# Readout of the second tile with values stationary, parts dealt evenly, and moved exponentials in a two-layer decoder trunk

## The chip, the cores and the metric

The kernel runs on one core of a Trainium2 chip. The metric is the device time of one execution in microseconds (us). TensorE (PE) multiplies matrices and turns tiles over (transposes), and loads each stationary operand with a weight load (PEld); VectorE (DVE), ScalarE (ACT) and GpSimd (POOL) work elementwise; SyncE (SP) issues the DMAs. Each engine takes its instructions in the order in which they are written and waits at an instruction until its semaphores are set. SBUF holds the tiles, PSUM has eight banks of 128 x 512 words into which PE writes.

## The reference, cut to what matters

```python
x <- LayerNorm(alpha * x + gated_deltanet(x))       # layer 1
shared keys and values of three branches from x      # compressed, selected, window
# layer 2, per head h of 16 and token t of 256 (heads in groups of 4 share keys and values):
q = rope(x @ wq); z = x @ wz (3 x 1024); gates = sigmoid(x @ wg)
o_b = softmax(q k_b^T, masked) v_b                   # b = compressed, selected, window
o = sum_b gates_b * o_b * silu(z_b)
x <- LayerNorm(alpha * x + o @ w_out)
```

With 256 tokens the selected and the window branch read the same 256 positions with different masks.

## The kernel before, in words

All products run in about 32 bits on PE: a projection is three products (high by high, high by low, low by high part), so a weight block is cast to its high part on ACT (`hi_*`, L181) and its low part is made on POOL (`lo_*`, L185).

The change lies in the second layer, from about 221 us of the span to its end. There the 256 tokens are two tiles of 128. The attention is cut into 24 units: a unit of tile 0 is a pair of heads (keys 0 to 127 only), a unit of tile 1 is one head (all 256 keys). The string `UNITS` gives their order, "0" for tile 0, "1" for tile 1. One unit is this chain: scores `s` (PE) into one of two score banks; `maxima` with the mask (DVE); `exps` (ACT) into `pt`; `transposes` of `pt` into the bank `ptp` (PE); copy to `PT` (ACT, `probs`); `readout` into the bank `op` (PE), where `PT` is stationary and the values with a column of ones (65 columns, `vtok`) stream, and a small product with `vbd` reads the compressed branch; five DVE instructions, here called the gated sums (L1418 to L1422), which divide by the sum in the ones column, multiply by gate and `zz`, and add the branches. `zz` is silu of z, made by `bz_done`: `th` on ACT, then `zz` on DVE.

Between scores and transposes of a unit, and between transposes of one and scores of the next, PE gets other work, so that the chain has time: `fill(n)` emits n parts of the projections (a part of `bz` or `bo` for tile 0 is six products of 512 columns, for the last sums of tile 1 twelve of 256). `FA` says how many parts stand ahead of a unit's exponentials, `FB` how many behind its readout and ahead of its transposes. The order on every engine is the order in which the program emits, `defer(n, f)` emits f at the n-th `step` after it, and each `fill` steps once for a part.

Two banks are shared with one buffer each: tag "t" (`tbank`: `ptp`, `qtp`, `tp_b`) and tag "o" (`obank`: `op`). Who asks for the bank waits until the last reader of its former content is done. The two score banks (`sbank`) also serve `gp` and `gq`, the gates' products.

The last steps: `merge` turns the summed heads over (`tp_b`) and splits them (`x1h`, `x1l`), then the parts of `bo` run, and the layer norm (`ln_part`, `ln_affine`) ends the kernel.

Of the kernel before, what the change touches and what calls it, by code (L numbers as in the profile page):

```python
# [9 lines left out]
F32 = mybir.dt.float32  # L10
# [24 lines left out]

FIRST = (1, 2)

UNITS = "001010101101101101111111"
FA = "3113111011210212044211123"
FB = "0211121311122110212111000"  # L40

PRE, TAIL = 4, 2
NEG = -1e30
# [50 lines left out]
def trunk(ctx: ExitStack, tc: tile.TileContext, I: dict, out: bass.AP):  # L94
# [9 lines left out]
    def defer(n, f):  # L104
        late.append([n, f])
# [802 lines left out]
    def ln_part(t, w, lo, ps, xin, dst):  # L908

        if lo == 0:  # L910
            stt[w, t] = [sm.tile([P, 4, 6], F32, tag="st", name=f"st_{w}{t}"), 0]
        st, n = stt[w, t]
        cc = slice(lo, lo + ps.shape[-1])
        V.scalar_tensor_tensor(dst[:, cc], xin[:, cc], SQRT2, ps, op0=ALU.mult, op1=ALU.add)
        V.bn_stats(st[:, n, :], dst[:, cc])
        stt[w, t][1] += 1

    def ln_mean(t, w):
# [6 lines left out]

    def ln_affine(t, w, b, dst, store=None, src=None):
        mv = ln_mean(t, w)
        if src:

            for c in range(2):  # L930
                V.scalar_tensor_tensor(src[c], src[c], mv[:, 0:1], lnp[w][:, c * 512:c * 512 + 512],
                                       op0=ALU.subtract, op1=ALU.mult)
            for c in range(2):
                cc = slice(c * 512, (c + 1) * 512)
                V.scalar_tensor_tensor(dst[:, cc], src[c], mv[:, 1:2], lnp[b][:, cc], op0=ALU.mult, op1=ALU.add)
            return
        for c in range(2):
            cc = slice(c * 512, (c + 1) * 512)
            V.scalar_tensor_tensor(dst[:, cc], dst[:, cc], mv[:, 0:1], lnp[w][:, cc], op0=ALU.subtract, op1=ALU.mult)
        for c in range(2):  # L940
            cc = slice(c * 512, (c + 1) * 512)
            V.scalar_tensor_tensor(dst[:, cc], dst[:, cc], mv[:, 1:2], lnp[b][:, cc], op0=ALU.mult, op1=ALU.add)
            if store:
                store(cc)
# [83 lines left out]
    def obank(name):  # L1028
        return pt_.tile([P, 512], F32, tag="o", name=name)
# [209 lines left out]
    def zview(t, c0, n):  # L1239
        i, o = c0 // 1536, c0 % 1536  # L1240
        return zz[2 * t + i][:, o:o + n]

    def need_z(t, cols):
        while not all((c, t) in zdone for c in range(-(-cols // 512))):
            fill(1)
# [12 lines left out]
    add_pairs(48)  # L1258
    S.copy(wgs[:, :, 0:48], wg)
    G.tensor_tensor(wgs[:, :, 48:96], wg, wgs[:, :, 0:48].bitcast(F32), op=ALU.subtract)  # L1260
    fill(1)
    r = q_split()
    fill(1)
    compressed_v()
    for i in range(4):
        if i:
# [54 lines left out]
    order0 = [(0, h) for h in range(0, 16, 2)]  # L1321
    order1 = [(1, h) for h in range(16)]
    units = [order0.pop(0) if k == "0" else order1.pop(0) for k in UNITS]
    S_, PT_, PTT, PC, PCT, MX, TP = {}, {}, {}, {}, {}, {}, {}
    cnt = {"n": 0}

    def scores(u):
# [26 lines left out]
    def exps(u):  # L1354
        t, h = u
        sp, mx = S_[u], MX[u]
        s4 = sp[:, :, 0:256].rearrange("p j (b k) -> p j b k", b=2)
        pt = PT_[u] = wk.tile([P, 2, 2, P], F32, tag="hl", name=f"pt{t}{h}", bufs=3)
        if t == 0 or h % 2 == 0:
            PC[t, h] = wk.tile([P, 2, 16], F32, tag="Pc", name=f"Pc{t}{h}", bufs=4)  # L1360
        Pc = PC[t, h - h % 2]
        if t == 0:
            for j in range(2):
                for b in range(2):
                    S.activation(pt[:, j, b, :], s4[:, j, b, :], AF.Exp, bias=mx[:, 2 * j + b:2 * j + b + 1])
                S.activation(Pc[:, j, :], sp[:, j, 256:272], AF.Exp, bias=mx[:, 4 + j:5 + j])
        else:
            for b in range(2):
                S.activation(pt[:, :, b, :], s4[:, :, b, :], AF.Exp, bias=mx[:, b:b + 1])  # L1369
            S.activation(Pc[:, h % 2, :], sp[:, 0, 256:272], AF.Exp, bias=mx[:, 4:5])  # L1370

    def transposes(u):
        t, h = u
# [16 lines left out]

    OP, summed = {}, set()

    def readout(t, h, half=None):

        g_ = h // 4
        if half != 1:
            need_z(t, (h + 2) * 192)
            OP[t] = obank(f"op{t}{h}")
        o3 = OP[t][:, 0:390].rearrange("p (r b d) -> p r b d", r=2, b=3)
        for r in range(2) if half is None else (half,):  # L1400
            PT = PTT[0, h] if t == 0 else PTT[1, h + r]
            for b in range(2):
                if t == 0:
                    PE.matmul(o3[:, r, 1 + b, :], PT[:, r, b, :], vt_[:, b, 0, g_, :], start=True, stop=True)
                else:
                    for j in range(2):
                        PE.matmul(o3[:, r, 1 + b, :], PT[:, j, b, :], vt_[:, b, j, g_, :], start=j == 0, stop=j == 1)  # L1407
        if half == 0:
            return
        PE.matmul(o3[:, :, 0, :], PCT[t, h], vbd[:, g_, :, :], start=True, stop=True)  # L1410
        rc = sm.tile([P, 2, 3], F32, tag="rc", name=f"rc{t}{h}")
        o4 = o3[:, :, :, 0:64]

        o_ = zview(t, h * 192, 128).rearrange("p (r d) -> p r d", r=2)

        def total():

            V.reciprocal(o3[:, :, :, 64], o3[:, :, :, 64])  # L1418
            V.tensor_tensor(rc, o3[:, :, :, 64], gt[:, t, h * 3:h * 3 + 6].rearrange("p (r b) -> p r b", b=3), op=ALU.mult)
            V.tensor_tensor(o4, o4, zview(t, h * 192, 384).rearrange("p (r b d) -> p r b d", r=2, b=3), op=ALU.mult)  # L1420
            V.tensor_tensor(o4, o4, rc[:, :, :, None].to_broadcast([P, 2, 3, 64]), op=ALU.mult)
            V.tensor_reduce(o_, o4.rearrange("p r b d -> p r d b"), axis=AX.X, op=ALU.add)  # L1422
            summed.add((t, h))

        defer(1, total)
# [17 lines left out]
    def bo_unit(t, c, part):  # L1443
        if part == 0:
            pb_[t, c] = [(sbank(f"pbl{c}{f}")[:, 0] if c else pjb(f"pbl{c}{f}")) for f in range(2)] if t else pjb(f"pbo{c}{t}")
        if t == 0 and c == 1 and part == 1:
            for nm in ("blw", "blb"):
                load_ln(nm, ring.tile([P, D], F32, tag="raw", name=nm, bufs=NRAW))
        x = x1[:, t, :]

        def store(cc):
            nc.sync.dma_start(out[t * P:(t + 1) * P, cc], x[:, cc])

        def done(lo, ps):
            ln_part(t, "blw", lo, ps, x, x)
            if lo + ps.shape[-1] == D:
                (ln_affine if t else ln_affine_aside)(t, "blw", "blb", x, store)

        if t == 1:

            for f in range(2):
                ps = pb_[t, c][f][:, 0:256]
                tm_part(ps, ("bo", 4 * c + part), part, t, *bT, cols=slice(256 * f, 256 * f + 256))
                if part == 3:
                    done(512 * c + 256 * f, ps)
            return
# [28 lines left out]
    for i in range(n + 1):  # L1495
        if i < n:
            scores(units[i])
        first = i < n and units[i][0] == 0 and not merges
        if first:

            maxima(units[i])
        if i:
            probs(units[i - 1])
        step()
        if i < n and not first:
            maxima(units[i])
        fill(int(FA[i]))
        advance()
        presplit()
        if i < n:  # L1510
            exps(units[i])
        if i:
            t, h = units[i - 1]
            if t == 0:
                readout(t, h)
                if h == 14:
                    cnt["t0"] = 1
                    merges += [lambda: merge0(0), lambda: merge0(1)] + ready
            else:

                if (units[i - 2] if h % 2 else units[i]) == (1, h ^ 1):
                    readout(t, h - h % 2, h % 2)
                elif h % 2:
                    readout(t, h - 1)
                if h % 4 == 3:
                    (merges if cnt["t0"] else ready).append(lambda g_=h // 4: merge1(g_))
        fill(int(FB[i]))
        if i < n:
            transposes(units[i])
    while len(merges) > 1:  # L1530
# [78 lines left out]
```

## Time and profile before

| | us |
|---|---|
| median of 3 runs | 386.9 (386.45 to 387.45) |
| profiled execution | 388.53 |
| its span, first to last instruction | 386.8 |
| PE busy | 374.7 (97%) |
| DVE, ACT, POOL busy | 223.6, 220.4, 247.1 |
| mean granted TensorE clock | 0.993 of full speed |

The profiled execution is 1.7 us longer than its span and 1.6 us longer than the median; busy shares are means over the whole span. Matmuls overlap in the records, so that the time that one adds to PE's row is read from start to start. In rows of the timeline, instructions of one kind that follow one another are one row with their count.

### The profile page before, as it was taken

What the parts mean: (1) busy time and instruction counts of PE and PEld (TensorE: products, weight loads), DVE (VectorE), ACT (ScalarE), POOL (GpSimd) and SP (SyncE); (2) the same over time, 40 slices, a digit from 0 to 9 for tenths busy, and PEclk for the clock granted to TensorE, in tenths of its full rate; (3) what the DMA queues carried; (4) which work ended last, traced back from release to release, by engine and by line L of the source; (5) the groups of instructions that cost most, each with busy time, mean ns of one, the idle gap of its engine ahead of it and who ended that gap; (6) DMA issues with size and microseconds to landing.
All of it is one profiled execution on the core that took longest, in us unless ns stands there. A gap on an engine that the chain in (4) does not pass through costs nothing.

```text
span 386.8 us, 7558 instructions
## 1 busy us (share of the span) xinstructions
PE 374.7 (97%) x2870; PEld 332.9 (86%) x2870; DVE 223.6 (58%) x591; ACT 220.4 (57%) x433; POOL 247.1 (64%) x157
## 2 busy tenths in 40 slices
PE   8899999999999999999999999999999999999991
PEld 6899999999888987888897878888888888878991
DVE  2777876588642543656542545754557456677726
ACT  4687785546854543535563567675664757456410
POOL 5499999837456747895854997474736547209051
PEclk9999999999999999999999999999999999999997
DMA  6776749845433316384545854433516143301011
GB/s 223 292 218 208 268 158 297 228 167 143 148 109 112 110 54 200 128 287 147 169 158 166 297 195 159 164 111 109 173 45 218 55 153 113 117 3 54 3 54 54
DMA packets 23476, 58.68 MB, mean 152 GB/s; under 512 B 6672, under 2 KB 9232, under 8 KB 23312
## 3 DMA queue, kind: packets, MB, share of 16 engines
q1 hardware_dynamic: 23232, 58.13, 45.1%
q8 instruction: 22, 0.36, 0.4%
q14 instruction: 14, 0.11, 0.1%
q10 hardware_dynamic: 144, 0.07, 0.1%
q0 software_dynamic: 64, 0.01, 0.0%
HBM read 55.96 MB, written 2.23 MB: 150 GB/s over the span
## 4 chain that ended last, share of the span: by engine, by line
PE 90%; DMA 3%; DVE 2%; POOL 1%; ACT 1%; issue 1%; POOLq 0%; SPq 0%; DVEq 0%
PE pbz L235 6%; PE pbz L233 6%; PE pbz L234 6%; PE op L1407 4%; PE s L1336 3%; PE ptp L1378 3%; PE pwz L233 2%; PE pk L217 2%; PE pwo L235 2%; PE pq L216 2%; PE pq L215 2%; PE pq L217 2%; PE pk L215 2%; PE pk L216 2%; PE pwo L234 2%; PE pwo L233 2%
## 5 line engine op out<-in xcount | busy, mean ns | idle before, releaser
L185 POOL TENSOR_TENSOR lo_bz<-raw_bz,hi_bz 128x1024 fp32r<-128x1024 f32 x24 | 56.8, 2392 | 36.2 <-ACT hi_bz L181 19.6
L185 POOL TENSOR_TENSOR lo_wqkv<-raw_wqkv,hi_wqkv 128x1024 fp32r<-128x1024 f32 x22 | 52.5, 2406 | 7.9 <-ACT hi_wqkv L181 6.1
L233 PE MATMUL pbz<-hi_bz,x1h 128*128 128x512 f32 x96 | 38.7, 403 | 0.0
L235 PE MATMUL pbz<-lo_bz,x1h 128*128 128x512 f32 x96 | 37.8, 394 | 0.0
L234 PE MATMUL pbz<-hi_bz,x1l 128*128 128x512 f32 x96 | 37.6, 392 | 0.0
L185 POOL TENSOR_TENSOR lo_bo<-raw_bo,hi_bo 128x1024 fp32r<-128x1024 f32 x8 | 18.9, 2387 | 21.7 <-ACT hi_bo L181 16.9
L185 POOL TENSOR_TENSOR lo_skv<-raw_skv,hi_skv 128x1024 fp32r<-128x1024 f32 x12 | 28.4, 2397 | 4.2 <-PE pskv L235 4.2
L185 POOL TENSOR_TENSOR lo_wz<-raw_wz,hi_wz 128x1024 fp32r<-128x1024 f32 x8 | 19.4, 2438 | 16.0 <-ACT hi_wz L181 10.6
L181 ACT CAST hi_bz<-raw_bz 128x1024 fp32r<-128x1024 f32 x24 | 25.3, 1052 | 2.5 <-POOL wgs L1260 1.6
L185 POOL TENSOR_TENSOR lo_bq<-raw_bq,hi_bq 128x1024 fp32r<-128x1024 f32 x8 | 19.1, 2393 | 11.6 <-ACT hi_bq L181 7.2
L185 POOL TENSOR_TENSOR lo_wo<-raw_wo,hi_wo 128x1024 fp32r<-128x1024 f32 x8 | 18.9, 2385 | 11.9 <-ACT hi_wo L181 11.9
L1385 ACT COPY PT<-ptp 128x512 f32<-128x512 f32 x24 | 14.1, 588 | 21.2 <-PE ptp L1378 21.2
L181 ACT CAST hi_wqkv<-raw_wqkv 128x1024 fp32r<-128x1024 f32 x22 | 22.8, 1043 | 2.4 <-DMA raw_wqkv<-in_wqkv 2.4
L235 PEld LDWEIGHTS pbz<-lo_bz,x1h 128*128 128x128 f32 x96 | 18.0, 188 | 4.3 <-POOL lo_bz L185 0.2
L234 PEld LDWEIGHTS pbz<-hi_bz,x1l 128*128 128x128 f32 x96 | 18.1, 188 | 2.8
L233 PEld LDWEIGHTS pbz<-hi_bz,x1h 128*128 128x128 f32 x96 | 18.1, 188 | 2.8
L1369 ACT ACTIVATE pt<-s,mx 128x256 f32<-128x256 f32 x32 | 13.4, 471 | 10.9 <-DVE mx L1352 8.7
L217 PE MATMUL pk<-xh,lo_wqkv 128*128 128x256 f32 x64 | 18.2, 285 | 0.9 <-POOL lo_wqkv L185 0.9
L215 PE MATMUL pk<-xh,hi_wqkv 128*128 128x256 f32 x64 | 18.6, 290 | 0.0
L215 PE MATMUL pq<-xh,hi_wqkv 128*128 128x256 f32 x64 | 18.5, 289 | 0.0
L216 PE MATMUL pk<-xl,hi_wqkv 128*128 128x256 f32 x64 | 18.1, 283 | 0.0
L217 PE MATMUL pq<-xh,lo_wqkv 128*128 128x256 f32 x64 | 18.1, 283 | 0.0
(362 smaller groups left out, 1257.9 us busy)
## 6 DMA issues: line engine op xcount, KB each, us to landing
raw_bz<-in_bz SPq DMA_DIRECT2D x24, 512.0 KB, 3.3
raw_wqkv<-in_wqkv SPq DMA_DIRECT2D x23, 512.0 KB, 4.4
raw_skv<-in_skv SPq DMA_DIRECT2D x12, 512.0 KB, 3.3
raw_wz<-in_wz SPq DMA_DIRECT2D x8, 512.0 KB, 3.9
raw_wo<-in_wo SPq DMA_DIRECT2D x8, 512.0 KB, 3.6
raw_bq<-in_bq SPq DMA_DIRECT2D x8, 512.0 KB, 3.6
raw_bo<-in_bo SPq DMA_DIRECT2D x8, 512.0 KB, 3.3
raw_w<-in_w SPq DMA_DIRECT2D x4, 512.0 KB, 3.3
```

The costliest lines, as they stand in the source:

```text
L181: S.copy(h, r)
L185: e.tensor_tensor(l, r, h.bitcast(F32), op=ALU.subtract)
L215: PE.matmul(ps[:, 0:T], wh[:, kt, :], ah[:, kt, :], start=kt == 0, stop=False)
L216: PE.matmul(ps[:, 0:T], wh[:, kt, :], al_[:, kt, :], start=False, stop=False)
L217: PE.matmul(ps[:, 0:T], wl[:, kt, :], ah[:, kt, :], start=False, stop=kt == 7)
L233: PE.matmul(ps, ah[:, kt, tt], wh[:, k4, cols], start=kt == 0, stop=False)
L234: PE.matmul(ps, al_[:, kt, tt], wh[:, k4, cols], start=False, stop=False)
L235: PE.matmul(ps, ah[:, kt, tt], wl[:, k4, cols], start=False, stop=kt == 7)
L1336: PE.matmul(sp[:, j, 0:n], lq, kk[:, hh // 4, c0:c0 + n], start=i == 0, stop=i == 1)
L1369: S.activation(pt[:, :, b, :], s4[:, :, b, :], AF.Exp, bias=mx[:, b:b + 1])
L1385: S.copy(PT.rearrange("p a b c -> p (a b c)"), TP[u])
L1407: PE.matmul(o3[:, r, 1 + b, :], PT[:, j, b, :], vt_[:, b, j, g_, :], start=j == 0, stop=j == 1)
```

## The change

It does six things.

1. `UNITS`, `FA` and `FB` are new tables: nearly every unit has one or two parts ahead of its readout and one behind.
2. The readout of tile 1 (`readout_rows`) has the values stationary (64 columns) and `PT` streaming (128 columns): eight products for a pair of heads, which fill the lower and upper half of the partitions of a "t" bank by turns. DVE copies the result to `oS`. In the next unit, behind its first part, `turn_back` turns `oS` over with two transposes into the "o" bank and adds the product with `vbd`.
3. The sums of the softmax of tile 1 come from the exponentials (`accum_out`, 48 instructions) in place of the ones column.
4. `exps` stands ahead of the weights' cast (`presplit`), and for units of tile 0 up to the merges right behind `maxima`, ahead of what `step` emits.
5. The first `q_split` stands ahead of two parts instead of between them.
6. For tile 1, the first 512 columns of the last sums stay in their two banks until the last layer norm has read them.

```diff
-UNITS = "001010101101101101111111"
-FA = "3113111011210212044211123"
-FB = "0211121311122110212111000"
+UNITS = "001101100111011100111111"
+FA = "3112121111111111111222213"
+FB = "0111111111111111101010100"
...
-        V.scalar_tensor_tensor(dst[:, cc], xin[:, cc], SQRT2, ps, op0=ALU.mult, op1=ALU.add)
-        V.bn_stats(st[:, n, :], dst[:, cc])
+        y = ps if dst is None else dst[:, cc]
+        V.scalar_tensor_tensor(y, xin[:, cc], SQRT2, ps, op0=ALU.mult, op1=ALU.add)
+        V.bn_stats(st[:, n, :], y)
...
-        for c in range(2):
-            cc = slice(c * 512, (c + 1) * 512)
-            V.scalar_tensor_tensor(dst[:, cc], dst[:, cc], mv[:, 0:1], lnp[w][:, cc], op0=ALU.subtract, op1=ALU.mult)
+        for c, y in enumerate(src):
+            cc = slice(c * 256, (c + 1) * 256)
+            V.scalar_tensor_tensor(dst[:, cc], y, mv[:, 0:1], lnp[w][:, cc], op0=ALU.subtract, op1=ALU.mult)
+        cc = slice(512, 1024)
+        V.scalar_tensor_tensor(dst[:, cc], dst[:, cc], mv[:, 0:1], lnp[w][:, cc], op0=ALU.subtract, op1=ALU.mult)
...
-    fill(1)
     r = q_split()
-    fill(1)
+    fill(2)
...
+            den = DEN[h - h % 2]
             for b in range(2):
-                S.activation(pt[:, :, b, :], s4[:, :, b, :], AF.Exp, bias=mx[:, b:b + 1])
-            S.activation(Pc[:, h % 2, :], sp[:, 0, 256:272], AF.Exp, bias=mx[:, 4:5])
+                S.activation(pt[:, :, b, :], s4[:, :, b, :], AF.Exp, bias=mx[:, b:b + 1],
+                             accum_out=den[:, h % 2, 1 + b:2 + b])
+            S.activation(Pc[:, h % 2, :], sp[:, 0, 256:272], AF.Exp, bias=mx[:, 4:5], accum_out=den[:, h % 2, 0:1])
...
+    def readout_rows(h):
+
+
+        g_ = h // 4
+        tb = tbank(f"ot{h}")
+        for r in range(2):
+            for j in range(2):
+                for b in range(2):
+                    PE.matmul(tb[64 * b:64 * b + 64, r * P:(r + 1) * P], vt_[:, b, j, g_, 0:64], PTT[1, h + r][:, j, b, :],
+                              start=j == 0, stop=j == 1)
+        oS = wk.tile([P, 2, P], F32, tag="oS", name=f"oS{h}", bufs=1)
+        V.tensor_copy(oS.rearrange("p a b -> p (a b)"), tb[:, 0:2 * P])
+        backs.append(lambda: turn_back(h, oS))
+
+    def turn_back(h, oS):
+        need_z(1, (h + 2) * 192)
+        op = OP[1] = obank(f"op1{h}")
+        o3 = op[:, 0:384].rearrange("p (r b d) -> p r b d", r=2, b=3)
+        for r in range(2):
+            PE.transpose(op[:, r * 192 + 64:r * 192 + 192], oS[:, r, :], ident)
+        PE.matmul(o3[:, :, 0, :], PCT[1, h], vbd[:, h // 4, :, 0:64], start=True, stop=True)
+        defer(1, lambda: gated(1, h, o3, DEN[h]))
...
+        if first:
+            exps(units[i])
         step()
         if i < n and not first:
             maxima(units[i])
-        fill(int(FA[i]))
+
+        k = 1 if merges else 0
+        if backs:
+            fill(1)
+            turn()
+            fill(int(FA[i]) - 1 - k)
+        else:
+            fill(int(FA[i]) - k)
         advance()
+        fill(k)
+        if i < n and not first:
+            exps(units[i])
         presplit()
-        if i < n:
-            exps(units[i])
         if i:
             t, h = units[i - 1]
             if t == 0:
-                readout(t, h)
+                readout(h)
...
-                if (units[i - 2] if h % 2 else units[i]) == (1, h ^ 1):
-                    readout(t, h - h % 2, h % 2)
-                elif h % 2:
-                    readout(t, h - 1)
+                if h % 2:
+                    readout_rows(h - 1)
```

In the changed kernel the gated sums are L1407 to L1411, the readout of tile 0 is L1422 and L1423, that of tile 1 L1436, the copy to `oS` L1439, the turning back L1447 and L1448, and the exponentials of tile 0 are L1369 and L1370.

The order on ACT at the start of the weave, before: the last two casts of queries, the table of the exponential with the gates' exponential, a weight block's cast, `th` of the first part, then the first unit's exponentials.

```order
L1224 CAST qT_2696<-qtp_3059 128x4x128
L1224 CAST qT_2696<-qtp_3064 128x4x128
L1310 ACT_TABLE_LOAD
L1310 ACTIVATE gq<-gq 128x96
L181 CAST hi_bz_3090<-raw_bz_2935 128x1024
L1236 ACTIVATE th_3101<-pbz_3004 128x512
L1365 ACTIVATE pt_3117<-s_3072,mx_3077 128x128 x2
L1366 ACTIVATE Pc_3118<-s_3072,mx_3077 128x16
L1365 ACTIVATE pt_3117<-s_3072,mx_3077 128x128 x2
L1366 ACTIVATE Pc_3118<-s_3072,mx_3077 128x16
```

And with the change:

```order
L1369 ACT_TABLE_LOAD
L1369 ACTIVATE pt_3081<-s_3072,mx_3077 128x128 x2
L1370 ACTIVATE Pc_3082<-s_3072,mx_3077 128x16
L1369 ACTIVATE pt_3081<-s_3072,mx_3077 128x128 x2
L1370 ACTIVATE Pc_3082<-s_3072,mx_3077 128x16
L1227 CAST qT_2696<-qtp_3059 128x4x128
L1227 CAST qT_2696<-qtp_3064 128x4x128
L1312 ACTIVATE gq<-gq 128x96
L181 CAST hi_bz_3098<-raw_bz_2935 128x1024
L1239 ACTIVATE th_3109<-pbz_3004 128x512
```

The table and the first unit's exponentials have moved ahead of the casts of the queries, the gates' exponential and `th`.

The order on PE around the scores of the last pair of tile 0 (`s_4030` before, `s_4019` after), before: the readout of a tile-1 pair (`op_4014`), the transposes of the unit ahead, then the scores; two parts and the transposes follow (rows 1715 to 1727, not shown).

```order
L1407 MATMUL op_4014<-vtok,PT_3871 128x65 x4
L1407 MATMUL op_4014<-vtok,PT_3973 128x65 x4
L1410 MATMUL op_4014<-vbd,PcT_2388 128x2x65
L1378 MATMUL ptp_4025<-ident,pt_4009 128x128 x4
L1336 MATMUL s_4030<-kh,qT_2696 128x272
L1336 MATMUL s_4030<-kl,qT_2696 128x272
```

With the change, from the last half of the part behind the scores:

```order
L233 MATMUL pbz_4042<-hi_bz_3622,x1h 128x512
L234 MATMUL pbz_4042<-hi_bz_3622,x1l 128x512
L235 MATMUL pbz_4042<-lo_bz_3623,x1h 128x512
L1447 MATMUL op_4049<-ident,oS_4005 128x128 x2
L1448 MATMUL op_4049<-vbd,PcT_2388 128x2x64
L1422 MATMUL op_4059<-vtok,PT_4028 128x65 x4
L1423 MATMUL op_4059<-vbd,PcT_2389 128x2x65
L1384 MATMUL ptp_4065<-ident,pt_4031 128x128 x4
L1386 MATMUL s_4019<-ident,Pc_4032 32x128
```

The turning back of a tile-1 pair (`op_4049`) and the readout of a tile-0 pair (`op_4059`) now stand side by side, and both ask for the one "o" bank.

The order on DVE at the same place, before: maxima of that unit, the gated sums of `op_4014`, maxima of the next unit.

```order
L1345 TENSOR_TENSOR s_4030<-s_4030,cb 128x2x272
L1346 TENSOR_REDUCE mx_4035<-s_4030 128x4
L1347 TENSOR_REDUCE mx_4035<-s_4030 128x2
L1418 RECIPROCAL op_4014<-op_4014 128x6
L1419 TENSOR_TENSOR rc_4024<-op_4014,gt 128x6
L1420 TENSOR_TENSOR op_4014<-op_4014,zz_3273 128x6x64
L1421 TENSOR_TENSOR op_4014<-op_4014,rc_4024 128x6x64
L1422 TENSOR_REDUCE zz_3273<-op_4014 128x128
L1349 TENSOR_TENSOR s_4072<-s_4072,cb 128x256
```

With the change, from the last of the maxima on:

```order
L1240 SCALAR_TENSOR_TENSOR zz_3598<-th_4039,pbz_3931 128x512
L1407 RECIPROCAL op_4049<-den_3883 128x6
L1408 TENSOR_TENSOR rc_4079<-op_4049,gt 128x6
L1409 TENSOR_TENSOR op_4049<-op_4049,zz_3922 128x384
L1410 TENSOR_TENSOR op_4049<-op_4049,rc_4079 128x384
L1411 TENSOR_REDUCE zz_3922<-op_4049 128x128
L1407 RECIPROCAL op_4059<-op_4059 128x6
L1408 TENSOR_TENSOR rc_4085<-op_4059,gt 128x6
L1409 TENSOR_TENSOR op_4059<-op_4059,zz_3598 128x6x64
L1410 TENSOR_TENSOR op_4059<-op_4059,rc_4085 128x6x64
L1411 TENSOR_REDUCE zz_3598<-op_4059 128x128
L1351 TENSOR_TENSOR s_4071<-s_4071,cb 128x256
```

DVE now has `zz` and then two runs of gated sums one behind the other, and the second run reads the bank that PE writes only when the first is done.

## Rows read from the trace of the kernel before

**Rows 1.** The page, part 4: shares of the chain that ended last, by engine.
```profile
PE 90%; DMA 3%; DVE 2%; POOL 1%; ACT 1%; issue 1%; POOLq 0%; SPq 0%; DVEq 0%
```

**Rows 2.** Windows: length; busy us of PE, PEld, DVE, ACT, POOL; granted clock; DMA.
```profile
232.00:332.00 100.00, 100.00 (x599) 87.21 (x598) 57.24 (x134) 63.85 (x142) 58.11 (x25) 1.00 0.40 132
332.00:346.00 14.00, 13.08 (x87) 10.83 (x86) 12.05 (x32) 7.19 (x21) 0.00 (x0) 1.00 0.10 39
```

**Rows 3.** Timeline, first units with a readout: start us, us, engine, line, operation, [idle before].
```profile
246.03 0.40 PE L233 MATMUL pbz<-hi_bz,x1h 128*128 128x512 f32 x1
...
247.41 1.00 PE L1404 MATMUL op<-vtok,PT 128*128 128x65 f32 x8
247.60 0.18 DVE L1347 TENSOR_REDUCE mx<-s 128x2 f32<-128x32 f32 x1
247.90 0.62 ACT L1365 ACTIVATE pt<-s,mx 128x128 f32<-128x128 f32 x2 [1.55 <-DVE mx L1347]
...
248.73 0.20 DVE L1418 RECIPROCAL op<-op 128x6 f32<-128x6 f32 x1 [0.94 <-PE op L1410]
...
249.07 0.30 ACT L1366 ACTIVATE Pc<-s,mx 128x16 f32<-128x16 f32 x1
...
250.12 0.60 ACT L1236 ACTIVATE th<-pbz 128x512 f32<-128x512 f32 x1 [0.75 <-PE pbz L235]
...
250.37 0.56 DVE L1422 TENSOR_REDUCE zz<-op 128x128 f32<-128x384 f32 x1
...
250.84 0.68 DVE L1237 SCALAR_TENSOR_TENSOR zz<-th,pbz 128x512 f32<-128x512 f32 x1
```

**Rows 4.** Timeline of PE, one readout of a pair of tile 1.
```profile
271.36 1.89 PE L1407 MATMUL op<-vtok,PT 128*128 128x65 f32 x16
273.09 0.44 PE L1410 MATMUL op<-vbd,PcT 128*128 128x130 f32 x2
...
273.60 0.40 PE L234 MATMUL pbz<-hi_bz,x1l 128*128 128x512 f32 x1
```

**Rows 5.** Timeline, a column-tiled block (L1150, the keys' and values' compression).
```profile
207.17 0.39 PE L235 MATMUL pbq<-lo_bq,x1h 128*128 128x512 f32 x1
...
207.48 1.72 PEld L1150 LDWEIGHTS hpT<-raw_w,C 128*61 128x61 f32 x32 [0.35 <-issue]
...
209.38 0.50 PE L233 MATMUL pbq<-hi_bq,x1h 128*128 128x512 f32 x1
...
209.72 0.39 PE L234 MATMUL pbq<-hi_bq,x1l 128*128 128x512 f32 x1
```

**Rows 6.** Timeline, the first unit of the weave: ACT and DVE.
```profile
239.68 1.07 ACT L1224 CAST qT<-qtp 128x512 fp32r<-128x512 f32 x2 [0.20 <-PE qtp L1223]
...
240.78 1.28 ACT L1310 ACT_TABLE_LOAD   x1
...
242.07 0.23 ACT L1310 ACTIVATE gq<-gq 128x96 f32<-128x96 f32 x1
...
243.93 0.24 DVE L1315 TENSOR_SCALAR gt<-gq,cb 128x16 f32<-128x16 f32 x1
```

**Rows 7.** Timeline, the first turning of queries (L1223).
```profile
223.38 0.66 PE L1223 MATMUL qtp<-ident,hlq 128*128 128x128 f32 x4 [0.54 <-DVE hlq L1048]
```

**Rows 8.** Timeline, small POOL operations in two layer norms, layer 1's and the last.
```profile
155.73 0.23 POOL L922 TENSOR_SCALAR mv_alw<-mv_alw 128x1 f32<-128x1 f32 x1 [3.05 <-DVE mv_alw L921]
...
156.04 0.57 POOL L923 TENSOR_TENSOR mv_alw<-mv_alw,mhalf 128x1 f32<-128x1 f32 x1
...
380.44 0.78 POOL L922 TENSOR_SCALAR mv_blw<-mv_blw 128x1 f32<-128x1 f32 x1 [6.70 <-DVE mv_blw L921]
381.30 0.93 POOL L923 TENSOR_TENSOR mv_blw<-mv_blw,mhalf 128x1 f32<-128x1 f32 x1
```

**Rows 9.** Busy time behind PE's last matmul, as in rows 2.
```profile
380.00:381.00 1.00, 0.00 (x0) 0.00 (x0) 0.93 (x3) 0.00 (x0) 0.56 (x1) 1.00 0.00 0
381.00:382.00 1.00, 0.00 (x0) 0.00 (x0) 0.80 (x2) 0.00 (x0) 0.92 (x2) 0.82 0.00 0
```

More of the change, by code (lines that the diff above doesn't have):

```diff
@@ L927, in ln_affine @@
         mv = ln_mean(t, w)
-        if src:
+        if src and not store:
             for c in range(2):
@@ L1323, in trunk @@
     units = [order0.pop(0) if k == "0" else order1.pop(0) for k in UNITS]
-    S_, PT_, PTT, PC, PCT, MX, TP = {}, {}, {}, {}, {}, {}, {}
+    S_, PT_, PTT, PC, PCT, MX, TP, DEN = {}, {}, {}, {}, {}, {}, {}, {}
     cnt = {"n": 0}
@@ L1360, in exps @@
             PC[t, h] = wk.tile([P, 2, 16], F32, tag="Pc", name=f"Pc{t}{h}", bufs=4)
+            if t:
+                DEN[h] = sm.tile([P, 2, 3], F32, tag="den", name=f"den{h}", bufs=3)
         Pc = PC[t, h - h % 2]
@@ L1391, in trunk @@
     OP, summed = {}, set()
-    def readout(t, h, half=None):
-        g_ = h // 4
[L1396 to L1401, printed above, removed]
-            for b in range(2):
[L1403 to L1425, printed above, removed]
@@ new lines, in gated @@
+    def gated(t, h, o4, den):
+        rc = sm.tile([P, 2, 3], F32, tag="rc", name=f"rc{t}{h}")
+        o_ = zview(t, h * 192, 128).rearrange("p (r d) -> p r d", r=2)
+        rd = OP[t][:, 0:390].rearrange("p (r b d) -> p r b d", r=2, b=3)[:, :, :, 64] if t == 0 else \
+            OP[t][:, 384:390].rearrange("p (r b) -> p r b", r=2)
+        V.reciprocal(rd, den)
+        V.tensor_tensor(rc, rd, gt[:, t, h * 3:h * 3 + 6].rearrange("p (r b) -> p r b", b=3), op=ALU.mult)
+        V.tensor_tensor(o4, o4, zview(t, h * 192, 384).rearrange("p (r b d) -> p r b d", r=2, b=3), op=ALU.mult)
+        V.tensor_tensor(o4, o4, rc[:, :, :, None].to_broadcast([P, 2, 3, 64]), op=ALU.mult)
+        V.tensor_reduce(o_, o4.rearrange("p r b d -> p r d b"), axis=AX.X, op=ALU.add)
+        summed.add((t, h))
@@ new lines, in readout @@
+    def readout(h):
+        g_ = h // 4
+        need_z(0, (h + 2) * 192)
+        OP[0] = obank(f"op0{h}")
+        o3 = OP[0][:, 0:390].rearrange("p (r b d) -> p r b d", r=2, b=3)
+        for r in range(2):
+            for b in range(2):
+                PE.matmul(o3[:, r, 1 + b, :], PTT[0, h][:, r, b, :], vt_[:, b, 0, g_, :], start=True, stop=True)
+        PE.matmul(o3[:, :, 0, :], PCT[0, h], vbd[:, g_, :, :], start=True, stop=True)
+        defer(1, lambda: gated(0, h, o3[:, :, :, 0:64], o3[:, :, :, 64]))
@@ new lines, in trunk @@
+    backs = []
+    def readout_rows(h):
[9 more added lines that the diff above has]
+        backs.append(lambda: turn_back(h, oS))
@@ L1428, in trunk, with turn @@
+    def turn_back(h, oS):
+        need_z(1, (h + 2) * 192)
+        op = OP[1] = obank(f"op1{h}")
+        o3 = op[:, 0:384].rearrange("p (r b d) -> p r b d", r=2, b=3)
+        for r in range(2):
+            PE.transpose(op[:, r * 192 + 64:r * 192 + 192], oS[:, r, :], ident)
+        PE.matmul(o3[:, :, 0, :], PCT[1, h], vbd[:, h // 4, :, 0:64], start=True, stop=True)
+        defer(1, lambda: gated(1, h, o3, DEN[h]))
+    def turn():
+        while backs:
+            backs.pop(0)()
     bT = x1h, x1l
@@ L1454, in done @@
         def done(lo, ps):
-            ln_part(t, "blw", lo, ps, x, x)
+            inb = t == 1 and lo < 512
+            ln_part(t, "blw", lo, ps, x, None if inb else x)
             if lo + ps.shape[-1] == D:
-                (ln_affine if t else ln_affine_aside)(t, "blw", "blb", x, store)
+                if t:
+                    ln_affine(t, "blw", "blb", x, store, [p[:, 0:256] for p in pb_[1, 0]])
+                else:
+                    ln_affine_aside(t, "blw", "blb", x, store)
         if t == 1:
@@ L1506, in trunk @@
             maxima(units[i])
-        fill(int(FA[i]))
+        k = 1 if merges else 0
[3 more added lines that the diff above has]
+            fill(int(FA[i]) - 1 - k)
+        else:
+            fill(int(FA[i]) - k)
         advance()
+        fill(k)
+        if i < n and not first:
+            exps(units[i])
         presplit()
-        if i < n:
-            exps(units[i])
         if i:
@@ L1533, in trunk @@
     add_bo(1, [(1, g_) for g_ in range(3)])
+    fill(1)
+    turn()
     fill(TAIL)
```

## The prediction

> **What bounds the kernel now.** I read the chain that ended last first: PE holds 90% of it [rows 1], so the end moves with PE alone, and other engines count only where PE waits for them. The windows come next. From 232 to 332 us, the body of the weave, PE has no idle microsecond at full clock, while DVE and ACT are busy for 57 and 64 of 100; the only gap of note is 14.00 - 13.08 = 0.92 us between 332 and 346 [rows 2]. So before, every chain from scores to transposes and from readout to gated sums is covered by PE work. What the change is worth is then two sums: PE time that it takes away, and covers that it makes shorter than the chains that they hide. The timeline gives the lengths of these chains, below.
>
> **PE time taken away.** A pair's readout of tile 1 stands from 271.36 to the next part's first product; that one starts 0.23 before 273.60, at 273.37: 2.01 us, of which the two `vbd` passes are 0.28 [rows 4]. (Products of 512 columns start 0.23 apart: six from 246.03 to 247.41 [rows 3]; a part is 1.38.) The new readout has 16 passes of 128 columns on 64 stationary columns. Nearest row: the column-tiled block L1150, with 61 stationary and 128 moving columns. From 207.40 (207.17 + 0.23) to 209.49 (209.72 - 0.23) it takes 2.09 us for 32 passes, whose weight loads are 1.72: 0.054 a pass, and 0.37 that belong to its entry and exit [rows 5]. Sixteen passes: 0.86 + 0.37 = 1.23. The turning back is two transposes of 128 columns, taken at the price of the two `vbd` passes, 0.28, and the `vbd` product itself, 0.28: 0.56. Together 1.79 against 2.01: -0.22 a pair, -1.8 for eight. Bounds: -0.59 a pair (-4.7) if entry and exit cost nothing; +2.2 in all if a pass costs 0.108 (1.73 / 16, what a pass with 128 stationary columns costs in rows 4): 16 x 0.108 + 0.56 - 2.01 = 0.28 a pair. I take -1.8, since L1150 has nearly the same shape.
>
> The Trainium skill bears on this in "TensorEngine Tiling (Array Packing)", section "When to Use Tiling": for a streamed side of at most 64 columns it advises to swap the operands and tile by columns, up to twice as fast. By that rule the 1.73 become 0.87, a pair costs 1.43, and the sum gains 4.7 instead of 1.8, which would end at 396.6. The same page's "Key Properties" says that a change of tiling mode drains the engine, and the 0.37 of the row agrees with that.
>
> Moving `q_split` ahead of both parts gives one more part to the chain that PE waits for at 223.38, -0.5 [rows 7]. The stretch of 0.92 has new tables; I count it as won, -0.9, since its waits are in the losses if they return. At the end the first layer-norm step reads banks while POOL makes the root: POOL's two steps took 0.78 and 0.93 beside a DVE that reads SBUF, 0.23 and 0.57 beside one that reads banks [rows 8]; half of that is to be had, as the third instruction still reads SBUF, and the products beside them go on: -0.3 (bounds 0 and -0.9). Sum of gains: -3.5.
>
> **Waits that it makes.** Let U be PE's time when a unit's scores have been issued. In the rows U is 246.03. Maxima end at U + 1.75, exponentials run from 247.90 to 249.37 (U + 3.34), a `th` is 0.60, a `zz` 0.68, and the gated sums from 248.73 to 250.93 are 2.20 [rows 3]. A turned pair is read by gated sums that release the "o" bank only when the last of the five is done; a tile-0 readout that follows on PE stands and waits, and with it all parts, transposes and scores behind it.
>
> *Last pair of tile 0* (the order of PE and DVE that is shown). DVE does maxima (U + 1.75), then `zz`, whose `th` stands behind the exponentials that were moved up: U + 3.34 + 0.60 = 3.94, with latencies U + 4.0; `zz` until U + 4.7; gated sums of the turned pair until U + 6.9. PE has one part and the turning back, 1.38 + 0.56 = U + 1.94. Stall 5.0.
>
> *Head pair 8 of tile 0*: the same two readouts side by side, with no `zz` between. The gated sums start when the turned pair is there, U + 2.1, and end at U + 4.3; PE stands since U + 1.94. Stall 2.4.
>
> *Head 2 of tile 1*: a part lies between the two. `th` of the part behind the scores ends at U + 2.1, `zz` at U + 2.85, gated sums at U + 5.05; PE is there at 1.38 + 0.56 + 1.38 = U + 3.3. Stall 1.8.
>
> *Head pair 6 of tile 0*: transposes want the "t" bank that the copy to `oS` must release. The copy stands behind maxima and that `zz`: U + 4.7, plus the copy, 0.2 to 0.56 by the DVE rows of 6 and 384 columns [rows 3], so U + 5.0. PE's cover is 1.38 + 1.23 + 1.38 = 4.0. Stall 1.0.
>
> *First unit.* Before, the table (1.28) was loaded while the maxima still ran, and the two casts of queries (1.07) were over before it [rows 6]. Now table and exponentials wait for the maxima, and the casts behind them: U + 1.75 + 0.1 + 1.28 + 1.47 = U + 4.6, casts until U + 5.7. The transposes need the "t" bank that the second cast frees; PE's three parts end at U + 4.1. Stall 1.6. The second scores take the bank of `gq`: its exponential (0.23) and DVE's steps (242.55, behind the maxima, to 244.17: 1.62 [rows 6]) end at U + 7.6, and PE is there at U + 5.7 + 0.5 = 6.2. Stall 1.3. Together 2.9.
>
> The Trainium skill, "ScalarE: Activation LUTs", section "What ACT_TABLE_LOAD costs", gives some 2.7 us with a drain for a load. By that figure this term would be 4.3 and the whole 1.4 more. Here the load is 1.28, and the next activation starts 0.01 behind it [rows 6], so the trace does not show the drain.
>
> *The rest.* Covers of tile-1 units with two parts (2.76) are near their chains; in the merges the exponentials queue behind casts on ACT; the 48 accumulated sums may cost ACT something that no row shows: nothing at least, and at most another small activation each, 0.15 (half of the 0.30 of the 16-column one [rows 3], whose start overlaps the one ahead), which three to a unit and 16 units is 7. Most units have some slack. Bounds 0 and 7, I take 2.5. Last, the clock: idle behind its last product, PE had a granted clock of 1.00 in 380 to 381 and of 0.82 in 381 to 382 [rows 9]. At the last pair it idles for 5.0 us in the middle of its work, so it may run at 1.2 instead of 2.4 GHz for a stretch behind that: bounds 0 and 2.5 (a stall's worth of work at half speed), I take 0.5.
>
> Losses: 5.0 + 2.4 + 1.8 + 1.0 + 2.9 + 2.5 + 0.5 = 16.1. Net 16.1 - 3.5 = 12.6. The profiled execution's span of 386.8 becomes 399.4, its time 388.53 becomes 401.1. The median stands 1.6 under that execution, so the forecast is 386.9 + 12.6 = 399.5.
>
> **The rivals.** (1) *Only the bank waits with nothing between bind* (last pair, pair 8, first unit); the others are half as long as I take them and the rest costs nothing: 5.0 + 2.4 + 2.9 + 1.4 - 3.5 = 8.2, or 5.3 if the tiling gives its full -4.7: 392 to 395. For it: 2.5 of the rest has no row. Against it: 1.8 and 1.0 are worked out like the others.
>
> (2) *The covers hold* (the other side). The "o" bank's release at the three places and the casts at the start do not make PE wait. Its price is then the gains alone, 386.9 - 3.5 = 383.4, and 380.5 if entry and exit of the column-tiled blocks cost nothing. It decides at the last pair: gated sums over by U + 2, when PE arrives, against U + 6.9; between the two is the whole sum. Before, the same kind of chain did stay hidden over 100 us [rows 2]. Against it: DVE cannot start these sums ahead of maxima and `zz`, and U is set by PE itself, so that no slack is carried from one unit to the next.
>
> (3) *The waits feed on each other*: the rest at 7, clock at 2.5: 399.5 + 4.5 + 2.0 = 406. For it: 5.0 us of idling. Against: only one stall is that long.
>
> **How the numbers follow.** The forecast's case, 395.5 to 403, has 0.68; rival 1, 389 to 395.5, 0.14; rival 3, over 403, 0.12; rival 2, 0.05; and 0.01 remains for something close to no change. The range leaves out rival 2 and the far end of rival 3: 389.5 to 404.5; its low end is rival 1 with the full tiling gain and a smaller first unit. About 0.3% (1.2 us) is what a measurement of this kernel tells from no change: faster 0.05, same 0.02, slower 0.93.
>
> **What would show it.** PE's waits name the sums' last step L1411 before L1422, about 5.0, 2.4 and 1.8 us long; PE's gap before the first transposes and the second scores of the weave is near 1.6 and 1.3; the table load begins after the first maxima; the passes of L1436 lie some 0.055 apart with 0.37 around them; the granted clock dips once, behind the long stall, if anywhere; POOL's two last steps get shorter; the wait at 223.38 goes. I am wrong if L1422 never waits for L1411, if stalls behind the first are much shorter than worked out because ACT's or DVE's work had been done earlier than the order lets me see, or if column-tiled passes cost over 0.1.

## The result and the profile after

The changed kernel takes 405.1 us (median of 6, 402.1 to 409.1) against 387.0 of before (median of 6); the ratio is 1.0456, 95% interval 1.0407 to 1.0505. The direction was forecast; 405.1 lies 0.6 above the range's end of 404.5, and the loss is 18.1 where 12.6 was forecast. The profiled execution took 407.22, its span is 405.5. The execution of 409.1 counts as a slow one and is left out of the ratio; the other five have a median of 404.0.

From the page, PE's busy time, then PE's row and the granted clock's row in 40 slices of some 10 us (9 is 90% or more):

```profile
PE 380.8 (94%) x2886; PEld 331.7 (82%) x2886; DVE 226.1 (56%) x600; ACT 223.5 (55%) x481; POOL 246.5 (61%) x157
...
PE   8999999999999999999999997989699995989992
...
PEclk9999999999999999999999998998989999799997
```

PE has some gaps now, and the clock's row, 9 or more in every slice of before but the last, has several dips. PE's waits in the weave (engine, line, the instruction that ended the wait: us in total, times, longest):

```profile
PE op L1422 <- DVE zz L1411: 9.1, 3, 4.9
PE ptp L1384 <- ACT pt L1374: 1.9, 3, 1.2
PE ptp L1384 <- ACT qT L1227: 1.4, 1, 1.4
PE s L1338 <- DVE gt L1317: 1.1, 1, 1.1
PE ptp L1384 <- DVE oS L1439: 0.9, 1, 0.9
```

Before, this view had 0.6 and 0.2 us in all. The first row is the wait at the "o" bank, three times: in the unit of the last pair of tile 0 4.87, and by the timeline 2.38 in that of pair 8 and 1.84 in that of head 2 of tile 1, the three that the forecast named. The third and fourth are the first unit, the fifth the copy to `oS`.

What the forecast did not have in this size is the clock. Windows of 1 us (length; busy us of PE, PEld, DVE, ACT, POOL with counts; granted clock; DMA share, GB/s), behind the first unit's waits, behind the wait of 1.84, and around those of 2.38 and of 4.87:

```profile
248.00:249.00 1.00, 1.00 (x4) 0.81 (x3) 0.78 (x2) 0.10 (x1) 0.05 (x1) 0.50 0.00 0
...
275.00:276.00 1.00, 1.00 (x5) 0.92 (x5) 0.18 (x1) 0.00 (x0) 0.52 (x1) 0.50 0.00 0
...
293.00:294.00 1.00, 0.54 (x5) 0.57 (x6) 0.32 (x1) 0.00 (x0) 0.00 (x0) 1.00 0.00 0
...
295.00:296.00 1.00, 1.00 (x5) 0.77 (x4) 0.90 (x4) 0.00 (x0) 0.00 (x0) 0.59 0.00 0
...
297.00:298.00 1.00, 1.00 (x6) 0.94 (x6) 0.05 (x1) 0.13 (x1) 0.00 (x0) 0.50 0.00 0
...
342.00:343.00 1.00, 0.00 (x0) 0.00 (x0) 0.93 (x3) 0.00 (x0) 0.96 (x1) 0.98 0.00 0
...
344.00:345.00 1.00, 1.00 (x5) 1.00 (x6) 0.00 (x0) 0.00 (x0) 0.39 (x1) 0.50 0.00 0
...
349.00:350.00 1.00, 1.00 (x4) 0.79 (x3) 0.93 (x4) 0.00 (x0) 0.00 (x0) 0.60 0.00 0
```

Behind the wait of 2.38, PE was at work again from 293.46, and only then the clock fell, to 0.50, and came back before 299. At the last pair it fell within the wait of 4.87 and stayed at 0.50 into the window from 349, some 5.8 us after PE had its next work at 344.00. The timeline's row for the wait of 2.38:

```profile
293.46 1.08 PE L1422 MATMUL op<-vtok,PT 128*128 128x65 f32 x8 [2.38 <-DVE zz L1411]
```

### The profile page after: what moved, and what is told of

It is laid out like the page before. It is cut to its first block, busy times and chain, and to the rows that moved or that the text cites. A ratio compares the mean times of both kernels' runs of the same rounds, so it can differ in the third digit from the quotient of the medians.

```text
span 405.5 us, 7639 instructions
## 1 busy us (share of the span) xinstructions
PE 380.8 (94%) x2886; PEld 331.7 (82%) x2886; DVE 226.1 (56%) x600; ACT 223.5 (55%) x481; POOL 246.5 (61%) x157
## 5 line engine op out<-in xcount | busy, mean ns | idle before, releaser
L233 PE MATMUL pbz<-hi_bz,x1h 128*128 128x512 f32 x96 | 40.9, 426 | 0.0
L235 PE MATMUL pbz<-lo_bz,x1h 128*128 128x512 f32 x96 | 39.3, 410 | 0.0
L234 PE MATMUL pbz<-hi_bz,x1l 128*128 128x512 f32 x96 | 39.0, 406 | 0.0
L1374 ACT ACTIVATE pt<-s,mx 128x256 f32<-128x256 f32 x32 | 14.9, 474 | 12.1 <-DVE op L1407 5.7
L1384 PE MATMUL ptp<-ident,pt 128*128 128x128 f32 x96 | 17.0, 293 | 4.7 <-ACT pt L1374 1.9
L1384 PEld LDWEIGHTS ptp<-ident,pt 128*128 128x128 f32 x96 | 12.1, 149 | 11.3 <-ACT pt L1374 6.2
L234 PEld LDWEIGHTS pbz<-hi_bz,x1l 128*128 128x128 f32 x96 | 19.0, 198 | 2.6
L1240 DVE SCALAR_TENSOR_TENSOR zz<-th,pbz 128x512 f32<-128x512 f32 x12 | 8.2, 686 | 20.3 <-ACT th L1239 20.3
L1422 PE MATMUL op<-vtok,PT 128*128 128x65 f32 x64 | 10.0, 309 | 9.1 <-DVE zz L1411 9.1
```

The costliest lines, as they stand in the source:

```text
L233: PE.matmul(ps, ah[:, kt, tt], wh[:, k4, cols], start=kt == 0, stop=False)
L234: PE.matmul(ps, al_[:, kt, tt], wh[:, k4, cols], start=False, stop=False)
L235: PE.matmul(ps, ah[:, kt, tt], wl[:, k4, cols], start=False, stop=kt == 7)
L1240: V.scalar_tensor_tensor(zz[i][:, (c % 3) * 512:(c % 3 + 1) * 512], th, 1.0, ps, op0=ALU.add, op1=ALU.mult)
L1384: PE.transpose(tp[:, (2 * j + b) * P:(2 * j + b + 1) * P], pt[:, j, b, :], ident)
L1422: PE.matmul(o3[:, r, 1 + b, :], PTT[0, h][:, r, b, :], vt_[:, b, 0, g_, :], start=True, stop=True)
```

## The experiments

Two theories stood. A: the forecast's waits are right, and what it missed is the clock, about 8 us in the profiled execution. B: the clock costs little, the miss lies in the accumulated sums and thin covers. "Clock lost" below is the sum over windows of 1 us, from 232 us to PE's last product, of 1 minus the granted clock: 8.5 in the changed kernel's profile (0.5 of it while PE idled), 0 in that of before.

**Exponentials at their old place** (the changed kernel, this alone undone):

```diff
-        if first:
-            exps(units[i])
         step()
...
         fill(k)
-        if i < n and not first:
-            exps(units[i])
         presplit()
+        if i < n:
+            exps(units[i])
```

> The changed kernel with the exponentials back at their old place, behind the parts and the weights' cast. Theory A (the forecast's waits are right and what it missed is the clock, about 8 us): the first unit's waits go (2.5 us and about 1.7 of half clock behind them), the wait for the copy of the turned tile goes (0.9), the long wait of the last pair shrinks from 4.9 to 2.8 with a part of its 3 us of clock: 405 becomes 397 to 398.5, and there is no fall of the clock in the first unit. Theory B (the miss lies in the accumulated sums and thin covers, the clock costs little): 405 becomes 399.5 to 401, the waits alone.

Measured: 397.8 us (median of 4), ratio 1.0285 (1.0261 to 1.0308). As A had it. The first unit's waits and the wait for the copy are gone, the longest wait at the "o" bank is 2.7 in place of 4.9. PE's waits:

```profile
PE op L1422 <- DVE zz L1411: 5.0, 2, 2.7
...
PE op L1422 <- ACT pt L1374: 1.8, 1, 1.8
```

The second row shown is the wait of 1.84 under another name: it has the length that it had, and stands at the same instruction. That wait and the one of 2.3 left the clock alone in this profile; the wait of 2.7 did not (windows as above):

```profile
335.00:336.00 1.00, 0.86 (x4) 0.89 (x5) 0.00 (x0) 0.00 (x0) 0.34 (x1) 0.50 0.00 0
...
340.00:341.00 1.00, 1.00 (x3) 0.79 (x3) 0.93 (x3) 0.00 (x0) 0.00 (x0) 0.50 0.00 0
```

The clock stayed at 0.50 for more than six microseconds behind a wait of 2.7. Clock lost: 3.4.

**Products that keep PE at work during the waits** (nothing taken away):

```diff
+    def warm(h):
+        k = {4: 6, 6: 9, 12: 20}.get(h, 0)
+        if k:
+            tb = tbank(f"wm{h}")
+            for _ in range(k):
+                PE.matmul(tb, x1h[:, 0, 0:P], x1h[:, 0:2, :].rearrange("p a b -> p (a b)"), start=True, stop=True)
...
             if t == 0:
+                warm(h)
                 readout(h)
```

> The changed kernel with 6, 9 and 20 products of 512 columns, whose result nobody reads, put in front of the three tile-0 readouts that wait (stalls of 1.8, 2.4 and 4.9 us; the products are 1.4, 2.1 and 4.6 us). Nothing is taken away, and PE has 8 us of work more. Theory A: the clock no longer falls at these three places, 6.3 us come back: 398.5 to 400, and the waits named there shrink to 0.3 to 0.5 each. Theory B: 405 to 406.

Measured: 400.95 us (median of 4), ratio 1.0368 (1.0347 to 1.0388): 4.1 us faster than the changed kernel with 8 us of PE work more. This falls between the two expectations, 0.95 above A's and 4 below B's, and only A has a gain at all. In the timeline and the windows at the last pair, 20 products, then the readout, at full clock:

```profile
336.32 4.82 PE L1433 MATMUL wm<-x1h 128*128 128x512 f32 x20
341.43 1.08 PE L1422 MATMUL op<-vtok,PT 128*128 128x65 f32 x8 [0.29 <-DVE zz L1411]
```

```profile
341.00:342.00 1.00, 0.71 (x6) 0.60 (x6) 0.28 (x1) 0.00 (x0) 0.86 (x1) 1.00 0.00 0
342.00:343.00 1.00, 1.00 (x11) 1.00 (x11) 0.18 (x1) 0.00 (x0) 0.00 (x0) 1.00 0.10 25
```

The three waits at the "o" bank are 1.1 us together, and the clock is lost in the first unit alone (1.7), where no free bank was at hand for such products. In the profiled executions the gain is 407.22 - 402.15 = 5.1. At half clock products of 512 columns start 0.43 apart (348.22 to 348.65, below) in place of 0.23, so a microsecond at 0.50, which is half a microsecond of clock lost, loses 0.47 of work, and the 6.3 of clock lost at the three places, with 0.5 of it idle left out already, are 5.9 by that reckoning. Of the 0.8 between 5.9 and 5.1, 0.3 lie ahead of the weave (first scores at 238.62 here, at 238.32 in the changed kernel's profile), and PE's starts lose the rest again behind the waits: 0.3 at the transposes behind the second place, 0.2 at the next readout behind the third. The expectation took the profiled execution's clock; a usual one loses less, as the next table shows.

The times of the changed kernel's executions (the five of the ratio) go with their mean granted clock, and so do those of the kernel with the exponentials alone (below):

| kernel | us at mean granted clock, each execution |
|---|---|
| changed | 402.1 at 0.985, 404.0 and 404.0 at 0.982, 406.2 at 0.977, 407.2 at 0.973 |
| exponentials alone | 391.5 at 0.995, 393.1 at 0.992, 394.3 at 0.987, 397.0 at 0.984 |

**The old readout in the changed kernel** (`readout` and `total` of before, no `accum_out`, no `turn`):

```diff
-                if h % 2:
-                    readout_rows(h - 1)
+                if (units[i - 2] if h % 2 else units[i]) == (1, h ^ 1):
+                    readout(t, h - h % 2, h % 2)
+                elif h % 2:
+                    readout(t, h - 1)
```

> The changed kernel with the readout of tile 1 of before and without accumulated sums; tables, exponentials, split and last sums as changed. Theory A: the three long waits of the tile-0 readout (9.1) and that for the copy (0.9) go with some 6 us of half clock behind them, the waits for the accumulating exponentials (1.9) too, and the old readout costs 1.8 more: 388 to 390, with the first unit's waits and clock dip still there. Theory B: the clock's part is small, so 394 to 396.

Measured: 391.8 us (median of 4), ratio 1.0121 (1.0102 to 1.0140). Of the 13.3 us that come back, A had 15 to 17 and B 9 to 11: the time lies between them, 1.8 above A's range and 2.2 below B's, and decides little by itself. A took the clock of the profiled execution, and its waits say what else A left out: the old readout has new waits in these tables, 1.7 us in all with two of 0.2 that are not shown:

```profile
PE op L1408 <- DVE zz L1426: 0.8, 2, 0.4
PE ptp L1380 <- ACT pt L1367: 0.5, 1, 0.5
```

The first unit's two waits are as they were, and the clock's only dip (1.7) is behind them.

**The two local edits alone** (the kernel before, `q_split` ahead of `fill(2)`, and half of the last sums in their banks, as in the diff of the change).

> The kernel before with only the two local edits: the first split of queries ahead of both parts, and half of tile 1's last sums kept in their banks. Theory A and the forecast: the wait of 0.54 at the first turning goes and POOL's root is 0.3 to 0.4 shorter: 386.1 against 387.0. Rival: the won half microsecond returns as a wait in the first unit (table and casts of queries), only the last sums count: 386.6.

Measured: 386.07 us (median of 12) against 386.78, ratio 0.9977 (0.9963 to 0.9992): -0.7, as expected. The wait for the first turning of queries is gone, and this version is faster than both kernels, than the one before by 0.3 to 1.4 us.

**The new readout without its long waits** (the changed kernel, exponentials at their old place, and other tables):

```diff
-UNITS = "001101100111011100111111"
-FA = "3112121111111111111222213"
-FB = "0111111111111111101010100"
+UNITS = "001101100111110100111111"
+FA = "3000201130111001132001133"
+FB = "1211102111100111111101000"
```

> The changed kernel with the exponentials back at their old place and other tables (UNITS 001101100111110100111111, other FA and FB), so that a part or more lies between every turning back and the next readout of tile 0. Theory A (the new readout is worth 1.8 us on PE, and what lost the time was only waits and the clock behind them): no wait over 1 us, no fall of the clock, 386.5 to 389.5. If the new readout costs by itself (copy, second use of both banks, accumulated sums): still above 391.

Measured: 388.1 us (median of 6), ratio 1.0037 (1.0025 to 1.0050). No wait is above 1 us and the clock is whole up to PE's last product. Nine tenths of the loss are gone with the same new readout, copies, turnings and accumulated sums. But it doesn't beat the version with the two local edits. Windows of that version, then of the retuned one:

```profile
239.00:300.00 61.00, 61.00 (x356) 52.93 (x355) 36.37 (x84) 38.59 (x92) 33.46 (x15) 1.00 0.39 132
300.00:377.00 77.00, 76.10 (x508) 67.58 (x506) 47.36 (x117) 40.74 (x93) 34.26 (x18) 1.00 0.20 69
```

```profile
239.00:300.00 61.00, 59.66 (x365) 49.55 (x363) 38.21 (x92) 40.27 (x110) 32.74 (x14) 1.00 0.36 123
300.00:377.00 77.00, 73.97 (x495) 62.59 (x496) 46.38 (x114) 42.93 (x122) 34.76 (x19) 1.00 0.21 76
```

From 239 to 377 PE idles for 0.9 us there and 4.4 here, while its last product starts at 377.0 there and 378.7 here, and its first scores at 238.6 and 238.3. PE's work is thus smaller by 3.5 - 1.7 - 0.3 = 1.5 us (forecast: 1.8), and small waits, of the new readout's longer chains in these tables, give back more than that:

```profile
PE ptp L1384 <- ACT pt L1374: 1.4, 2, 0.9
PE ptp L1384 <- DVE oS L1439: 1.2, 2, 0.6
PE ptp L1384 <- ACT Pc L1376: 0.6, 1, 0.6
```

**The same without accumulated sums** (the sums taken as ones):

```diff
-                DEN[h] = sm.tile([P, 2, 3], F32, tag="den", name=f"den{h}", bufs=3)
+                DEN[h] = ones6
...
-                S.activation(pt[:, :, b, :], s4[:, :, b, :], AF.Exp, bias=mx[:, b:b + 1],
-                             accum_out=den[:, h % 2, 1 + b:2 + b])
+                S.activation(pt[:, :, b, :], s4[:, :, b, :], AF.Exp, bias=mx[:, b:b + 1])
...
```

> The kernel of the retuned tables without accumulated sums: the exponentials write none, and the softmax's sums of tile 1 are taken as ones (that part of the computation is left out). The accumulator's read adds 0.09 behind each exponential in the trace of the changed kernel, 0.28 on a unit's chain. Theory: only units without slack feel it, 0.5 to 1 us in all. Rival (the sums carry the shortfall of the forecast): 3 us or more.

Measured: 387.3 us, ratio 1.0013 (0.9996 to 1.0029), 0.8 below the kernel with them; the two intervals overlap a little. B's main term is small in these tables; in the changed kernel's own it was not measured.

**The exponentials moved up, alone** (the kernel with the two local edits and the change's order of `exps`).

> The kernel before with the two local edits and the exponentials moved up as in the change; readout and tables of before. Theory: the first unit's two waits, 1.4 and 1.1, come back and a clock dip of about 1.7 behind them, and later casts on ACT run behind the exponentials, so that a product waits for its weights once (about 2): 386.1 becomes 390 to 392.5. Rival (moving them up only costs together with the new readout): 386 to 387.

Measured: 393.7 us (median of 4), ratio 1.0185 (1.0139 to 1.0231), 7.7 above the kernel without this edit. The waits are those expected:

```profile
PE pbz L235 <- POOL lo_bz L185: 1.7, 1, 1.7
PE ptp L1380 <- ACT qT L1227: 1.4, 1, 1.4
PE s L1338 <- DVE gt L1317: 1.1, 1, 1.1
```

The time is above the expected 390 to 392.5. The profiled execution, 391.5, has these waits and no fall of the clock at all; the other three have a lower mean clock (table above). The four lie 5.5 us apart, and by their clocks some 4 of that is the clock (an estimate: 0.984 of 395.2 us against 0.995 of 389.8, times 0.93). So the same code pays between nothing and about 4 us of clock behind its waits; where the rest of the 5.5 lies is not shown.

## Why the prediction was wrong, point by point

**The step that failed** is the term for the clock: 0.5 with bounds 0 and 2.5, on the ground that only the stall of 5.0 was long enough; the prediction's sign was one dip of the clock, if any. In the profiled execution the clock fell behind all four groups of waits: the first unit's, 1.84, 2.38 and 4.87. It lost 8.0 while PE worked, by the spacing of products 8.0 x 0.93 = 7.4 us of work: some 1.6 behind each of the first three groups, which the term had at nothing, and 2.7 at the last pair, above the bound of 2.5. The only row for it was the kernel's end, where the clock fell between two and three microseconds after the last product. With 7.4 in place of 0.5 the forecast is 406.4, by the profiled execution's clock. The execution of 404.0, with a clock of 0.982, lost some 4.6 us of work (an estimate: 0.018 of its span of 402.3 us less 0.006 of the 385 us of a usual execution of before, times 0.93), which makes 403.6. The products that filled the waits show this by intervention, not only by rows.

The sum closes in the profiled executions. From the weave's first scores to PE's last product it is 240.28 to 378.67 before and 238.32 to 397.75 after, 21.0 us more, where the forecast's terms for this stretch were 16.1 - 1.8 - 0.9 = 13.4. Of the 7.6 that it lacked, the clock is 6.9 (7.4 - 0.5). Its waits were not what it lacked: PE idles for 165.00 - 149.94 = 15.1 us from 232 to 397, where the forecast's waits with its rest were 15.6. The last 0.7 or so were not found.

```profile
232.00:397.00 165.00, 149.94 (x911) 124.58 (x910) 88.27 (x213) 87.93 (x241) 72.25 (x34) 0.95 0.26 87
```

The Trainium skill speaks of it in "TensorE: Matmul & The Clock Gate", section "HAM oscillation — how this bites in real kernels": waits that come again and again between bursts of products bring the slow clock back each time. The dips at four places of the trace agree; the profiled execution of the exponentials alone, with three waits of 1.1 to 1.7 and no dip, shows that not every such wait does it. The forecast had weighed neither.

**The waits** were right: 5.0 forecast for the last pair and 4.87 measured, 2.4 and 2.38, 1.8 and 1.84, 1.0 and 0.9 for the copy, 2.9 and 2.5 for the first unit. The timeline of the last pair shows the chain as it was added up: turning back on PE over by 339.1, `th` behind the exponentials, `zz`, the last of the gated sums, and only then the readout; the two last rows are products at half clock.

```profile
338.74 0.39 PE L1448 MATMUL op<-vbd,PcT 128*128 128x128 f32 x2
...
340.40 0.63 ACT L1239 ACTIVATE th<-pbz 128x512 f32<-128x512 f32 x1
...
341.06 0.69 DVE L1240 SCALAR_TENSOR_TENSOR zz<-th,pbz 128x512 f32<-128x512 f32 x1 [2.11 <-ACT th L1239]
...
343.30 0.56 DVE L1411 TENSOR_REDUCE zz<-op 128x128 f32<-128x384 f32 x1
...
344.00 1.94 PE L1422 MATMUL op<-vtok,PT 128*128 128x65 f32 x8 [4.87 <-DVE zz L1411]
...
348.22 0.63 PE L233 MATMUL pbz<-hi_bz,x1h 128*128 128x512 f32 x1
...
348.65 0.63 PE L234 MATMUL pbz<-hi_bz,x1l 128*128 128x512 f32 x1
```

**The first unit**: the table's load begins when the maxima are done and the exponentials follow it by 0.02. No drain of the load shows, and the two waits behind it are 2.5 in all, under the 2.9 of the forecast.

```profile
240.48 0.18 DVE L1349 TENSOR_REDUCE mx<-s 128x2 f32<-128x32 f32 x1
...
240.76 1.28 ACT L1369 ACT_TABLE_LOAD   x1 [3.21 <-DVE mx L1349]
...
242.06 0.63 ACT L1369 ACTIVATE pt<-s,mx 128x128 f32<-128x128 f32 x2
```

**The new readout** is as priced. Its block lasts from 265.10 to 266.33 (products on both sides start 0.23 from their neighbours), 1.23 forecast and measured (seven of the eight blocks take 1.22 to 1.23); the turning back from 270.14 to 270.59, 0.45 where 0.56 was taken. Half of the old 1.73 would have been 0.87; the passes alone have that, and entry and exit add the 0.37 of [rows 5]. By these rows a pair wins 2.01 - 1.68 = 0.33, 2.6 for eight, where the retuned kernel's balance above gives 1.5; the 1.1 between the two were not found.

```profile
264.87 0.40 PE L235 MATMUL pbz<-lo_bz,x1h 128*128 128x512 f32 x1
265.20 1.09 PE L1436 MATMUL ot<-PT,vtok 128*64 128x128 f32 x16
...
266.56 0.40 PE L234 MATMUL pbz<-hi_bz,x1l 128*128 128x512 f32 x1
...
269.91 0.39 PE L235 MATMUL pbz<-lo_bz,x1h 128*128 128x512 f32 x1
270.14 0.38 PE L1447 MATMUL op<-ident,oS 128*128 128x128 f32 x2
...
270.82 0.39 PE L234 MATMUL pbz<-hi_bz,x1l 128*128 128x512 f32 x1
```

**The rest**, 2.5 with bounds 0 and 7: by PE's idle time it was 15.1 - 9.1 - 2.5 - 0.9 = 2.6. The waits for exponentials of tile 1 are 1.9 of it, in three places, of which the accumulated sums can be a part only (0.8 in the retuned kernel). That the guess of 2.5 fits is luck: no row stood behind it.

**The gains at both ends** were right: the first split and the last sums together -0.8 forecast (0.5 + 0.3), -0.7 measured. POOL's root beside a DVE that reads banks takes 0.22 and 0.57, as in the first two of [rows 8]:

```profile
399.56 0.22 POOL L923 TENSOR_SCALAR mv_blw<-mv_blw 128x1 f32<-128x1 f32 x1 [6.16 <-DVE mv_blw L922]
399.86 0.57 POOL L924 TENSOR_TENSOR mv_blw<-mv_blw,mhalf 128x1 f32<-128x1 f32 x1
```

The profiled execution of before, 388.53, stands 1.5 above the median of its kernel, so sums that are made against its span are that much uncertain. Of the rivals, the one whose waits feed on each other came out at 406, near the measured time, by luck: its rest was 7 where 2.6 was measured, and its clock of 2.5 a third of what it was. The covers held at none of the places named, and the waits that rival 1 took as half as long (1.8 and 1.0) came at full length.

## What to carry to other kernels

Price a stall of PE twice: the wait itself, and the clock behind it. Here 1.8 to 4.9 us of waiting cost up to another 3 us of work each, differently from one execution to the next, so that a kernel whose executions mostly lay within 0.5% spread by over 1%. Before two producers share a one-buffer bank, put the reader's whole chain (here `th`, `zz` and five gated sums) between them on PE, and look at what each in-order engine has queued ahead of that chain; products saved on PE (1.5 us here) can be worth less than the cover that they were. Where a wait can't be removed, products that nobody reads may win time (4.1 us here).

## What the runs showed of the hardware that was not expected

The clock can fall after PE is at work again (293.46 against 295, above), and behind one wait of 2.7 us it stayed at 0.50 for over 6 us while waits of the same kind, 1.8 and 2.3, were followed by no fall in the same execution. What decides whether a wait is followed by a fall is not shown by these runs. An accumulated sum on ACT is an instruction of its own in the trace, 0.19 to 0.2 us long, which moves the next activation's start by 0.09 (two such exponentials start 0.37 apart without it in the kernel before, 0.46 with it):

```profile
301.55 0.47 ACT L1374 ACTIVATE pt<-s,mx 128x256 f32<-128x256 f32 x1 [2.46 <-PE op L1423]
...
301.93 0.19 ACT L1374 ACTIVATION_READ_ACCUMULATOR pt<-s,mx 128x1 f32 x1
302.02 0.47 ACT L1374 ACTIVATE pt<-s,mx 128x256 f32<-128x256 f32 x1
```
